# Ranked experts of a mixture layer in a mixed order: two-block places between three-block places

## The chip, the core and the metric

The kernel runs on one core of one Trainium2 chip, as one launch that computes the whole reference. The metric is device time in microseconds of that launch; the median of three runs stands for the kernel.

## The reference, cut to what matters

Two decoder layers run over 256 tokens of width 1024. Each has a mixer of three attention branches, a cross-attention, and a channel mixer. The channel mixer of the second layer is a mixture of 8 experts, of which each token uses the best 2:

```
logits = (t @ w_router)
top_val, top_idx = lax.top_k(logits, TOP_K)                  # TOP_K = 2
combine = sum(one_hot(top_idx, 8) * softmax(top_val)[..., None])
for e in range(8):
    out = out + combine[:, e:e+1] * (silu(t @ w_gate[e]) * (t @ w_up[e])) @ w_down[e]
```

Each expert has three float32 matrices: gate and up (1024 x 3584) and down (3584 x 1024), 42 MiB together. All 8 experts are needed, so 336 MiB are read in this part of the program, whatever the tokens do. A final RMSNorm ends the program.

## The kernel before

The first layer, the attention of both layers and the router come first. From about 757 us on, the program is the expert part, and this is the only part that the change touches.

**Places.** The experts are worked through in 8 places. Place 0 is always expert 0. The other seven experts are ranked by their number of tokens (order_experts: `place` is a count of the experts that have more), and places 1 to 7 take them by rank. A place has a fixed size, `CAPS[i]`: the first five places have room for 96 tokens (three blocks of 32), the last three for 64 (two blocks). If an expert had more tokens than its place, a loop behind the program's end (`overflow`) would compute the rest; otherwise it is skipped. The matrices of a place are found at run time: `ids` holds the expert's number, SyncE loads it into a register, and the DMA addresses are formed with it.

**One place.** An expert is worked in four groups of 1024, 1024, 1024 and 512 of the 3584 inner columns. `gate_up` (L962) multiplies the gathered tokens `hg` by the gate and up matrices into one PSUM bank per block (`ps_gu0` to `ps_gu2`): 96 matmul calls for a full group with three blocks, 64 with two. The profile has two records for each of these calls. ScalarE and VectorE form silu(gate) * up (`act_group`). `down` (L1000) multiplies the result of the group before by the down matrix into `ps_ey` (48 or 32 calls for a full group). So TensorE does gate/up of group g, then down of group g - 1, and so on across the border of two places. When the last down of a place is done, `scatter` (L1022) brings its result back to the token rows, in the middle of the next place's second group. `back` (L943, `ps_c`) makes the map for that, and `gather` (L916, `ps_hg`) picks the tokens of two places at a time, once for places 0 and 1, 2 and 3, 4 and 5, 6 and 7.

**The weights.** Each weight transfer moves a tile of 1 MiB (`raw`), 42 tiles for each place: per group 8 tiles for gate and up (4 in the last group) and 4 for down (2 in the last). All are issued by SyncE from one queue in one fixed order. The tiles live in 15 buffers, used in turn:

```
RAW1, RAW2, RAW3 = 3, 4, 8
    def raw_tile(self):
        pool = self.raws.pop(0)
        self.raws.append(pool)
        return pool.tile([P, 2048], F32, tag="raw", name="raw")
```

A transfer waits for two things: the last matmul that reads the tile 15 earlier must be done, and (eight semaphores in turn) the transfer 8 earlier must have landed. SyncE issues in order, so a waiting transfer holds all that are behind it. What the size of a place changes is how many matmuls read a tile, and so how soon its buffer comes free; the bytes are the same for each place.

Of the kernel before, what the change touches and what calls it, by code (L numbers as in the profile page):

```python
# [14 lines left out]
ALU = mybir.AluOpType  # L15
# [3 lines left out]
P = 128  # L19
D = 1024  # L20
KC = D // P
S = 256
# [8 lines left out]


TB = 32
CAPS = (96, 96, 96, 96, 96, 64, 64, 64)
BIG = sum(c == 96 for c in CAPS)

GROUPS = ((0, 1024), (1024, 1024), (2048, 1024), (3072, 512))

# [9 lines left out]
class Trunk:  # L48
# [744 lines left out]
    def numbers(self):  # L793

        m = N_EXP - 1
        self.num, self.numT = (self.rank.tile([P, m, m], F32, name=n) for n in ("num", "numT"))
        for a, p in ((self.num, [[0, m], [1, m]]), (self.numT, [[1, m], [0, m]])):
            self.nc.gpsimd.iota(a, pattern=p, base=1, channel_multiplier=0, allow_small_or_imprecise_dtypes=True)

    def order_experts(self, ps):  # L800

        nc = self.nc
        m = N_EXP - 1
        shape = [P, m, m]

        def small(name, shape=shape, dt=F32):
            return self.rank.tile(shape, dt, name=name)

        cnt = small("cnt", [P, N_EXP])
        nc.vector.tensor_copy(cnt, ps)  # L810
        lj = cnt[:, None, 1:].to_broadcast(shape)
        le = cnt[:, 1:, None].to_broadcast(shape)
        gt, eq = small("cgt"), small("ceq")
        nc.vector.tensor_tensor(gt, lj, le, op=ALU.is_gt)
        nc.vector.tensor_tensor(eq, lj, le, op=ALU.is_equal)
        nc.vector.tensor_tensor(eq, eq, self.lt[:, :m, :m], op=ALU.mult)
        nc.vector.tensor_tensor(gt, gt, eq, op=ALU.add)

        place = small("place", [P, N_EXP])
        nc.vector.memset(place[:, 0:1], 0.0)  # L820
        nc.vector.tensor_reduce(place[:, 1:], gt, axis=AX.X, op=ALU.add)
        nc.vector.tensor_scalar(place[:, 1:], place[:, 1:], 1.0, None, op0=ALU.add)

        self.at = small("at")
        nc.vector.tensor_tensor(self.at, place[:, None, 1:].to_broadcast(shape), self.numT, op=ALU.is_equal)
        self.pos2 = small("pos2", [P, NT, N_EXP])
        self.by_place(self.pos2, self.pos)
        ids = small("ids", [P, m])
        tmp = self.rank.tile(shape, F32, tag="bp", name="bp", bufs=2)
        nc.vector.tensor_tensor(tmp, self.at, self.num, op=ALU.mult)  # L830
        nc.vector.tensor_reduce(ids, tmp, axis=AX.X, op=ALU.add)
        self.ids = small("idi", [P, m], I32)
        nc.vector.tensor_copy(self.ids, ids)

        self.cap = small("cap", [P, N_EXP])
        nc.vector.tensor_scalar(self.cap, place, BIG - 0.5, -(CAPS[0] - CAPS[-1]), op0=ALU.is_gt, op1=ALU.mult)
        nc.vector.tensor_scalar(self.cap, self.cap, float(CAPS[0]), None, op0=ALU.add)
        nc.vector.tensor_tensor(cnt, cnt, self.cap, op=ALU.subtract)
        cm = small("cm", [P, 1])
        nc.vector.tensor_reduce(cm, cnt, axis=AX.X, op=ALU.max)  # L840
        nc.vector.tensor_scalar(cm, cm, float(CAPS[0]), None, op0=ALU.add)
        self.cnt = small("cnti", [P, 1], I32)
        nc.vector.tensor_copy(self.cnt, cm)
# [53 lines left out]
    def gather(self, i0):  # L897

        nc = self.nc
        caps = CAPS[i0:i0 + 2]  # L900
        n = sum(caps)
# [24 lines left out]
    def back(self, i):  # L926

        nc = self.nc
        big = CAPS[i] == 96
        m = 3 if big else 1  # L930
# [131 lines left out]
    def overflow(self, wg, wu, wd, out):  # L1062

        nc, tc = self.nc, self.tc
        n = nc.values_load(self.cnt[0:1, 0:1], min_val=0, max_val=S)
        with tc.If(n > CAPS[0]):
            with ExitStack() as st:
                sb = st.enter_context(tc.tile_pool(name="ov", bufs=1))
                raws = st.enter_context(tc.tile_pool(name="ovraw", bufs=2))
                ps1 = st.enter_context(tc.tile_pool(name="ovps1", bufs=2, space=PSUM))  # L1070
                ps2 = st.enter_context(tc.tile_pool(name="ovps2", bufs=1, space=PSUM))
                with tc.For_i(0, N_EXP, 1) as e:
                    for first in range(0, S - CAPS[-1], P):
                        self.overflow_expert(e, first, wg, wu, wd, sb, raws, ps1, ps2)
                    for a in (self.pos, self.cw, self.cap[:, None, :]):
                        tmp = sb.tile([P, NT, N_EXP - 1], F32, tag="shift", name="shift")[:, :a.shape[1]]
                        nc.vector.tensor_copy(tmp, a[:, :, 1:])
                        nc.vector.tensor_copy(a[:, :, :N_EXP - 1], tmp)
                self.finish(out)
# [191 lines left out]
```

## Time and profile before

| | |
|---|---|
| median of 3 runs | 1649.74 us (1647.7 to 1650.09) |
| profiled execution, own time | 1652.03 us |
| its span, first to last instruction | 1650.2 us |
| TensorE busy | 1591.9 us (96%) |
| VectorE, ScalarE, GpSimd busy | 621.3, 476.7, 72.0 us |
| DMA | 473.63 MB, mean 287 GB/s |

The busy share of TensorE is an average over the whole program, and a matmul's end in the profile is modelled: a TensorE that is 96% busy can still wait for weights in one part of the program. So the stretches have to be read one by one, and in each the rate of the transfers beside the work of TensorE.

### The profile page before, as it was taken

Reading aid. Unit: us, or ns where it says so; the run is one execution under the profiler, and the core shown is the slowest. Engines: PE = TensorE matmul, PEld = TensorE weight load, DVE = VectorE, ACT = ScalarE, POOL = GpSimd, SP = SyncE. Lnnn points to the kernel's source line nnn. Section 1 sums busy time; section 2 is a strip of 40 time slices with the busy share of each in tenths; the row PEclk is TensorE's granted clock in tenths of the full one; section 3 lists DMA queues with packets and bytes.
Section 4 is the critical chain, followed back from the end, with each engine's and each line's share of the span. In section 5 each row is a group of like instructions: output and inputs, shape, how many; then the busy total and the mean of one; then the engine's idle time right before and its main releaser. Section 6 shows DMA issues by size and latency. Waiting matters only on the chain.

```text
span 1650.2 us, 31391 instructions
## 1 busy us (share of the span) xinstructions
PE 1591.9 (96%) x13510; PEld 1003.7 (61%) x13510; DVE 621.3 (38%) x1150; ACT 476.7 (29%) x814; POOL 72.0 (4%) x106
## 2 busy tenths in 40 slices
PE   8999999999999999998999999999999999988885
PEld 7989998999999899973454343343343333322222
DVE  6656665655576666643212112202203122111111
ACT  6556556544455575532000000001001001000001
POOL 2003100000011021000000000000000000000000
PEclk9999999999999999997999999999999999999998
DMA  8445764655344355738999899998999999999996
GB/s 258 130 117 172 234 201 129 208 193 179 128 140 142 103 180 193 266 103 329 376 412 388 336 403 367 393 410 314 399 404 363 402 411 408 411 412 407 413 409 239
DMA packets 188768, 473.63 MB, mean 287 GB/s; under 512 B 8976, under 2 KB 99408, under 8 KB 174288
## 3 DMA queue, kind: packets, MB, share of 16 engines
q1 hardware_dynamic: 188592, 471.56, 76.7%
q8 instruction: 108, 1.77, 0.4%
q14 instruction: 36, 0.29, 0.1%
q10 hardware_dynamic: 32, 0.01, 0.0%
HBM read 470.49 MB, written 1.05 MB: 286 GB/s over the span
## 4 chain that ended last, share of the span: by engine, by line
PE 85%; DMA 13%; DVE 1%; ACT 0%; issue 0%; SPq 0%; POOL 0%; POOLq 0%; DVEq 0%; ACTq 0%
PE ps_gu L962 26%; PE ps_ey L1000 13%; DMA raw<-in_moe_up_dram 8%; DMA raw<-in_moe_down_dram 4%; PE ps_gate L127 3%; PE ps_gate L125 3%; PE ps_gate L126 3%; PE ps_fu L126 1%; PE ps_fg L126 1%; PE ps_fu L125 1%; PE ps_fg L125 1%; PE ps_fg L127 1%; PE ps_fu L127 1%; PE acc L125 1%; PE acc L126 1%; PE acc L127 1%
## 5 line engine op out<-in xcount | busy, mean ns | idle before, releaser
L962 PE MATMUL ps_gu<-raw,hg 128*32 128x512 f32 (+1 forms) x5376 | 572.3, 541 | 22.7 <-DMA raw<-in_moe_up_dram 18.3
L962 PEld LDWEIGHTS ps_gu<-raw,hg 128*32 128x32 f32 x5376 | 199.8, 110 | 362.7 <-issue 295.8
L74 DVE TENSOR_TENSOR wl<-raw,wh 128x1024 fp32r<-128x1024 f32 x214 | 268.3, 1262 | 159.3 <-ACT wh L72 159.2
L978 DVE TENSOR_TENSOR sl<-ps_gu,tmp 64x256 f32<-64x256 f32 (+1 forms) x168 | 66.2, 394 | 620.3 <-ACT tmp L974 617.9
L1000 PE MATMUL ps_ey<-raw,aT 128*32 128x512 f32 x2352 | 281.5, 593 | 7.0 <-DMA raw<-in_moe_down_dram 7.0
L72 ACT ACTIVATE wh<-raw 128x1024 fp32r<-128x1024 f32 x214 | 225.1, 1058 | 198.6 <-PE ps_gate L127 38.9
L974 ACT ACTIVATE tmp<-ps_gu 64x512 f32<-64x512 f32 (+1 forms) x84 | 44.9, 535 | 654.5 <-PE ps_gu L962 628.9
L1000 PEld LDWEIGHTS ps_ey<-raw,aT 128*32 128x32 f32 x2352 | 89.0, 110 | 175.7 <-issue 147.1
L127 PE MATMUL ps_gate<-tLmix,wh 128*128 128x256 f32 x384 | 109.3, 285 | 0.0
L125 PE MATMUL ps_gate<-tHmix,wh 128*128 128x256 f32 x384 | 109.2, 284 | 0.0
L126 PE MATMUL ps_gate<-tHmix,wl 128*128 128x256 f32 x384 | 108.8, 283 | 0.0
L127 PEld LDWEIGHTS ps_gate<-tLmix,wh 128*128 128x128 f32 x384 | 72.6, 189 | 2.1 <-issue 1.3
L126 PEld LDWEIGHTS ps_gate<-tHmix,wl 128*128 128x128 f32 x384 | 72.3, 188 | 1.0 <-issue 0.8
L125 PEld LDWEIGHTS ps_gate<-tHmix,wh 128*128 128x128 f32 x384 | 72.0, 188 | 0.9 <-issue 0.7
L126 PE MATMUL ps_fu<-tHffn,wl 128*128 128x256 f32 x176 | 49.9, 283 | 0.0
L126 PE MATMUL ps_fg<-tHffn,wl 128*128 128x256 f32 x176 | 49.9, 283 | 0.0
L127 PE MATMUL ps_fg<-tLffn,wh 128*128 128x256 f32 x176 | 49.7, 283 | 0.0
L127 PE MATMUL ps_fu<-tLffn,wh 128*128 128x256 f32 x176 | 49.7, 282 | 0.0
L125 PE MATMUL ps_fu<-tHffn,wh 128*128 128x256 f32 x176 | 49.6, 282 | 0.0
L125 PE MATMUL ps_fg<-tHffn,wh 128*128 128x256 f32 x176 | 49.5, 281 | 0.0
L979 DVE STREAM_TRANSPOSE aT<-sl 128x256 f32<-128x256 f32 (+1 forms) x84 | 47.7, 586 | 2.0
L1024 DVE SCALAR_TENSOR_TENSOR x<-ps_sc,cw,x 128x512 f32<-128x512 f32 x32 | 22.5, 747 | 54.2 <-PE ps_sc L1022 54.2
(388 smaller groups left out, 2376.3 us busy)
## 6 DMA issues: line engine op xcount, KB each, us to landing
raw<-in_moe_gate_dram SPq DMA_DIRECT2D x112, 1024.0 KB, 9.9
raw<-in_moe_up_dram SPq DMA_DIRECT2D x112, 1024.0 KB, 9.9
raw<-in_moe_down_dram SPq DMA_DIRECT2D x112, 1024.0 KB, 9.4
raw<-in_w_in_dram SPq DMA_DIRECT2D x41, 1024.0 KB, 5.3
raw<-in_ffn_gate_dram SPq DMA_DIRECT2D x11, 1024.0 KB, 5.4
raw<-in_ffn_up_dram SPq DMA_DIRECT2D x11, 1024.0 KB, 5.4
raw<-in_ffn_down_dram SPq DMA_DIRECT2D x11, 1024.0 KB, 4.9
raw<-in_w_mix_out_dram SPq DMA_DIRECT2D x8, 1024.0 KB, 5.2
```

Source lines behind the costliest of these rows:

```text
L72: a = nc.scalar.activation(wh, raw, AF.Copy)
L74: b = nc.vector.tensor_tensor(wl, raw, wh.bitcast(F32), op=ALU.subtract)
L125: ms = [nc.tensor.matmul(out, lh, rh, start=first, stop=False), nc.tensor.matmul(out, ll, rh, start=False, stop=False), nc.tensor.matmul(o ...
L126: nc.tensor.matmul(out, ll, rh, start=False, stop=False),
L127: nc.tensor.matmul(out, lh, rl, start=False, stop=last)]
L962: nc.tensor.matmul(ps[b][TB * q:TB * q + TB, :w].rearrange("p (s c) -> p s c", s=2), gT[:, k, TB * b:TB * b + TB], src[q // 2][:, k % nk, ...
L974: nc.scalar.activation(tmp[64:, :w], ps[b][:64, :w], AF.Silu)
L978: nc.vector.tensor_tensor(sl[64 * s:64 * s + 64, :w // 2], ps[b][64:, c], tmp[64:, c], op=ALU.mult)
L979: nc.vector.transpose(aT[:, :n, TB * b:TB * b + TB], sl[:, :w // 2].rearrange("p (r i) -> p i r", i=n))
L1000: nc.tensor.matmul(y[m][TB * q:TB * q + TB, :], aT[:, i0 + j, TB * b:TB * b + TB], raw[:, j * D + 512 * half:j * D + 512 * half + 512], st ...
L1024: nc.vector.scalar_tensor_tensor(xc, ps, self.cw2[:, t, i:i + 1], xc, op0=ALU.mult, op1=ALU.add)
```

## The change

The seven ranked places no longer take the ranks in falling order. A list gives the rank that each place takes, and the sizes follow the ranks: the four largest ranked experts (and expert 0) still have three blocks, the three smallest two.

```diff
-CAPS = (96, 96, 96, 96, 96, 64, 64, 64)
-BIG = sum(c == 96 for c in CAPS)
+RANKS = (4, 0, 1, 5, 2, 3, 6)
+BIG = 5
+CAPS = (96,) + tuple(96 if r < BIG - 1 else 64 for r in RANKS)
...
-        for a, p in ((self.num, [[0, m], [1, m]]), (self.numT, [[1, m], [0, m]])):
-            self.nc.gpsimd.iota(a, pattern=p, base=1, channel_multiplier=0, allow_small_or_imprecise_dtypes=True)
+        self.nc.gpsimd.iota(self.num, pattern=[[0, m], [1, m]], base=1, channel_multiplier=0,
+                            allow_small_or_imprecise_dtypes=True)
+        for i, r in enumerate(RANKS):
+            self.nc.gpsimd.memset(self.numT[:, i, :], r + 1.0)
...
-        nc.vector.tensor_scalar(self.cap, place, BIG - 0.5, -(CAPS[0] - CAPS[-1]), op0=ALU.is_gt, op1=ALU.mult)
+        nc.vector.tensor_scalar(self.cap, place, BIG - 0.5, -(CAPS[0] - min(CAPS)), op0=ALU.is_gt, op1=ALU.mult)
...
-                    for first in range(0, S - CAPS[-1], P):
+                    for first in range(0, S - min(CAPS), P):
```

The sizes of places 0 to 7 become 96, 64, 96, 96, 64, 96, 96, 64. The two-block places are now 1, 4 and 7 instead of 5, 6 and 7. `numT` is the table against which an expert's rank is compared to find its place; it is now filled row by row. The pairs that `gather` takes become 160, 192, 160 and 160 columns wide instead of 192, 192, 160 and 128.

On TensorE, at the first gate/up group of place 1, these rows stood before, behind the last down rows of place 0's third group (`ps_ey0` and `ps_ey1` are the two result banks of a three-block place, `raw` with a number is one weight tile, `hg` the gathered tokens):

```order
L1000 MATMUL ps_ey1_8481<-raw_9030,aT_8862 32x512 x4
L1000 MATMUL ps_ey0_8480<-raw_9030,aT_8862 32x512 x4
L962 MATMUL ps_gu0_9073<-raw_9076,hg_8270 32x512 x2
L962 MATMUL ps_gu0_9073<-raw_9078,hg_8270 32x512 x2
L962 MATMUL ps_gu1_9074<-raw_9076,hg_8270 32x512 x2
L962 MATMUL ps_gu1_9074<-raw_9078,hg_8270 32x512 x2
L962 MATMUL ps_gu2_9075<-raw_9076,hg_8270 32x512 x2
L962 MATMUL ps_gu2_9075<-raw_9078,hg_8270 32x512 x2
```

And these stand at the same point of TensorE's queue in the changed kernel:

```order
L1003 MATMUL ps_ey1_8487<-raw_9036,aT_8868 32x512 x4
L1003 MATMUL ps_ey0_8486<-raw_9036,aT_8868 32x512 x4
L965 MATMUL ps_gu0_9079<-raw_9081,hg_8276 32x512 x2
L965 MATMUL ps_gu0_9079<-raw_9083,hg_8276 32x512 x2
L965 MATMUL ps_gu1_9080<-raw_9081,hg_8276 32x512 x2
L965 MATMUL ps_gu1_9080<-raw_9083,hg_8276 32x512 x2
```

The third bank is gone: each weight tile of place 1 is read by two thirds of the matmuls.

At the first group of place 6, TensorE's queue before had these rows, behind the down rows of place 5, which has one result bank:

```order
L1000 MATMUL ps_ey0_12438<-raw_12867,aT_12760 32x512 x8
L1000 MATMUL ps_ey0_12438<-raw_12877,aT_12760 32x512 x8
L962 MATMUL ps_gu0_12910<-raw_12912,hg_12445 32x512 x2
L962 MATMUL ps_gu1_12911<-raw_12912,hg_12445 32x512 x2
L962 MATMUL ps_gu0_12910<-raw_12914,hg_12445 32x512 x2
L962 MATMUL ps_gu1_12911<-raw_12914,hg_12445 32x512 x2
```

In the changed kernel the same point of TensorE's queue, between places 5 and 6, reads:

```order
L1003 MATMUL ps_ey1_12030<-raw_12630,aT_12462 32x512 x4
L1003 MATMUL ps_ey0_12029<-raw_12630,aT_12462 32x512 x4
L965 MATMUL ps_gu0_12673<-raw_12676,hg_12037 32x512 x2
L965 MATMUL ps_gu1_12674<-raw_12676,hg_12037 32x512 x2
L965 MATMUL ps_gu2_12675<-raw_12676,hg_12037 32x512 x2
L965 MATMUL ps_gu0_12673<-raw_12678,hg_12037 32x512 x2
L965 MATMUL ps_gu1_12674<-raw_12678,hg_12037 32x512 x2
L965 MATMUL ps_gu2_12675<-raw_12678,hg_12037 32x512 x2
```

Places 5 and 6 now have the third block that places 1 and 4 gave up. SyncE's queue, with all 336 weight transfers, reads the same in both kernels row for row, and TensorE's queue is the same up to the first gather.

## Rows read from the trace of the kernel before

**Rows 1.** The page: TensorE's clock and transfer rate in 40 slices; the end chain.

```profile
PEclk9999999999999999997999999999999999999998
...
GB/s 258 130 117 172 234 201 129 208 193 179 128 140 142 103 180 193 266 103 329 376 412 388 336 403 367 393 410 314 399 404 363 402 411 408 411 412 407 413 409 239
...
PE 85%; DMA 13%; DVE 1%; ACT 0%; issue 0%; SPq 0%; POOL 0%; POOLq 0%; DVEq 0%; ACTq 0%
```

**Rows 2.** Windows: length, busy us by engine (instructions), TensorE clock, DMA share, GB/s.

```profile
745.00:761.00 16.00, 11.12 (x45) 6.96 (x44) 11.14 (x54) 5.03 (x11) 2.90 (x10) 0.50 0.83 321
900.00:925.00 25.00, 25.00 (x218) 10.50 (x214) 6.68 (x18) 4.32 (x9) 0.00 (x0) 1.00 0.73 264
925.00:1400.00 475.00, 475.00 (x4646) 172.66 (x4642) 87.84 (x187) 36.51 (x71) 0.00 (x0) 1.00 0.99 389
1400.00:1625.00 225.00, 196.39 (x1668) 64.16 (x1660) 31.14 (x64) 11.28 (x22) 0.00 (x0) 1.00 1.02 411
1125.00:1150.00 25.00, 25.00 (x186) 10.85 (x182) 5.81 (x12) 2.96 (x7) 0.00 (x0) 1.00 0.75 285
1500.00:1525.00 25.00, 18.72 (x216) 7.61 (x210) 2.04 (x6) 0.75 (x2) 0.00 (x0) 1.00 1.03 406
1625.00:1650.00 25.00, 9.88 (x73) 2.63 (x72) 5.96 (x9) 3.97 (x9) 3.58 (x5) 0.77 0.34 132
```

**Rows 3.** Timeline of TensorE, three-block places: start, length, line, count, idle before.

```profile
814.50 20.83 PE L962 MATMUL ps_gu<-raw,hg 128*32 128x512 f32 x192
835.10 10.53 PE L1000 MATMUL ps_ey<-raw,aT 128*32 128x512 f32 x96
845.40 10.59 PE L962 MATMUL ps_gu<-raw,hg 128*32 128x256 f32 x192
...
866.06 20.83 PE L962 MATMUL ps_gu<-raw,hg 128*32 128x512 f32 x192
886.66 5.38 PE L1000 MATMUL ps_ey<-raw,aT 128*32 128x512 f32 x48
...
895.41 0.97 PE L1022 MATMUL ps_sc<-yH,cT 128*128 128x512 f32 x3
...
1013.92 0.96 PE L1022 MATMUL ps_sc<-yH,cT 128*128 128x512 f32 x3
...
1128.24 0.97 PE L1022 MATMUL ps_sc<-yH,cT 128*128 128x512 f32 x3
```

**Rows 4.** Timeline of TensorE, first two-block place (place 5).

```profile
1380.74 13.92 PE L962 MATMUL ps_gu<-raw,hg 128*32 128x512 f32 x128
1394.48 7.05 PE L1000 MATMUL ps_ey<-raw,aT 128*32 128x512 f32 x64
1401.35 7.11 PE L962 MATMUL ps_gu<-raw,hg 128*32 128x256 f32 x128
```

**Rows 5.** Timeline of TensorE, places 6 and 7.

```profile
1440.50 0.73 PE L1022 MATMUL ps_sc<-yH,cT 64*128 64x512 f32 x3 [0.70 <-ACT yH L226]
...
1478.43 4.45 PE L962 MATMUL ps_gu<-raw,hg 128*32 128x512 f32 x32 [0.65 <-DMA raw<-in_moe_up_dram]
1483.54 4.46 PE L962 MATMUL ps_gu<-raw,hg 128*32 128x512 f32 x32 [0.66 <-DMA raw<-in_moe_up_dram]
...
1547.57 0.73 PE L1022 MATMUL ps_sc<-yH,cT 64*128 64x512 f32 x3 [0.70 <-ACT yH L226]
...
1632.83 1.92 PE L1000 MATMUL ps_ey<-raw,aT 128*32 128x512 f32 x16 [0.47 <-DMA raw<-in_moe_down_dram]
```

**Rows 6.** The tile raw on SyncE's queue, 950 to 975 us, then 1450 to 1500 us.

```profile
DMA to landing us min/median/max: 7.5/9.8/10.2
...
DMA to landing us min/median/max: 13.9/19.8/20.5
```

**Rows 7.** Waits of SyncE's queue, 690 to 1650 us: total us, times, longest.

```profile
SPq L113 <- PE ps_gu L962: 248.2, 72, 10.2
SPq L113 <- PE ps_ey L1000: 154.9, 83, 7.9
SPq L992 <- PE ps_gu L962: 142.8, 53, 5.9
```

**Rows 8.** The gathers in the chain that ended last: start, length, tile, count.

```profile
908.47 2.85 PE ps_hg L916 x24
...
1367.66 2.83 PE ps_hg L916 x24
```

**Rows 9.** Timeline of GpSimd around the number tables.

```profile
659.11 0.27 POOL L798 IOTA numT<- 128x49 f32 x1
694.12 1.06 POOL L173 TENSOR_TENSOR varcrs<-sscrs 128x2 f32<-128x2 f32 x1 [34.74 <-ACT junk L165]
```

## The prediction, made before the changed kernel was run

> **What bounds the kernel now.** I read the page's slices first. From the twentieth slice on (about 784 us) the transfer rate lies near 400 GB/s, with dips to 336, 367, 314 and 363 up to the thirty-first, and then, without a dip, at 402 to 413 [rows 1]. The chain that ended last puts 85% on TensorE and 13% on DMA [rows 1], so both matter, each in its own stretch. The windows show which where. From 925 to 1400 us TensorE is busy for all 475 us and the transfers run at 389 GB/s. From 1400 to 1625 us TensorE is busy for 196.39 of 225 us and the transfers run at 411 GB/s, with a share of 1.02 [rows 2]. The reader is to see two stages with different limits. In the three-block places TensorE is the bound and the transfers are held back; in the two-block places at the end the transfers are the bound and TensorE waits.
>
> The waits agree. SyncE's queue waited 248.2, 154.9 and 142.8 us for matmuls that still read a buffer [rows 7], and TensorE's waits for weights stand in the two-block places, 0.65 us and more ahead of each pair of tiles [rows 5].
>
> **Three speeds.** All follow from starts in the timelines.
> - A three-block place reads the 8 tiles of a gate/up group in 835.10 - 814.50 = 20.60 us, and 4 down tiles in 10.30 us [rows 3]: 2.575 us a tile, 42 x 2.575 = 108.2 us a place. With scatter, map and gather a place takes 1013.92 - 895.41 = 118.5 us, without a gather 1128.24 - 1013.92 = 114.3 us [rows 3]. So the side work is 6.1 us, and 4.2 us more with a gather.
> - A two-block place, when nothing is late, reads 8 tiles in 1394.48 - 1380.74 = 13.74 us and 4 in 6.87 us [rows 4]: 1.717 us a tile, 72.1 us a place. Its side work is between nothing and the 6.1 us of a three-block place: 72.1 to 78.2 us.
> - The transfers, when nothing holds them, bring 42 tiles in 1547.57 - 1440.50 = 107.07 us [rows 5]: 2.549 us a tile, which is 411 GB/s.
>
> So against the transfers a three-block place is 7.3 or 11.4 us too slow, and a two-block place 29 to 35 us too fast. What evens this out is the 15 buffers. In the three-block places a transfer lands 9.8 us after its issue [rows 6], which is 9.8 / 2.575 = 3.8 tiles; the other 11.2 tiles lie ready, worth 11.2 x 2.549 = 28.5 us of transfers. In the drained state it takes 19.8 us [rows 6], 7.8 tiles, and nearly nothing lies ready. Before, the buffers are full through five places and can store nothing more, while each scatter and gather stops the transfers (285 GB/s from 1125 to 1150 us [rows 2]). Then they drain once, and places 6 and 7 run at the transfers' pace.
>
> **The change part by part.**
>
> The order. Place 0 is as before, and its buffers are full. Place 1 has two blocks: it drains 29 to 35 us, about what is stored, so TensorE waits 0 to 6 us there. Places 2 and 3 give back 11.4 + 7.3 = 18.7 us, less than the 28.5 us of room, so the buffers never fill and no transfer is held back. Place 4 drains again, and TensorE waits 10 to 16 us; places 5 and 6 store 18.7 us again; place 7 drains and waits 10 to 16 us. From place 1 on, the transfers run without a stop. Then the time saved is the time in which they were held back before:
> - 925 to 1400 us: 475 x (1 - 389/411) = 25.4 us [rows 2]. Another count goes by tiles. What was moved after 925 us is 475 x 389 + 225 x 411 + 25 x 132 thousand bytes per microsecond [rows 2], less 1.6 MB of output and final gain: 279 MB, 266 tiles. At 2.549 us they need 678 us, and the last one was waited for until 1632.83 [rows 5], 707.8 us later: 29.5 us. That count holds the few microseconds between the last byte and the matmul, which stay. I take 25.4 and keep 29.5 as the bound.
> - 900 to 925 us: the dip at the border of places 0 and 1 costs 25 x (1 - 264/411) = 8.9 us [rows 2]. The first group of place 1 starts at 866.06 [rows 3] and will take 13.7 instead of 20.6 us, so 8 buffers come free 6.9 us earlier, and the transfers have that much queued when the dip comes. Between 6.7 and 8.9 us is saved; I take 8.0.
>
> The work of TensorE. Five places of three blocks and three of two: the same number of matmuls, scatters and maps. The gathers are 160, 192, 160, 160 wide instead of 192, 192, 160, 128; 24 of their matmuls take 2.85 us at 192 columns and 2.83 us at 128 [rows 8]. Nothing is gained or lost.
>
> The queues. SyncE's order is unchanged, so no transfer stands behind another that it did not stand behind before; only the moments at which buffers come free move. Of TensorE's queue the small moves of scatter calls by a few matmuls cost at most the 0.70 us for which `yH` was waited [rows 5] at seven borders, 0 to 5 us, and lie under the transfers: TensorE still has 20 to 38 us of waiting from places 1, 4 and 7.
>
> The tables. One iota of 0.27 us becomes seven fills. Bounded by that iota from above and zero from below they cost 0 to 1.9 us, of which nothing counts: GpSimd has nothing to do for 34.74 us behind it [rows 9]. Without that cover they would cost those 1.9 us once. The changed arguments of `cap` and of the loop have the same values as before.
>
> The sum: 25.4 + 8.0 = 33.4 us less. The profiled execution took 1652.03 us around a span of 1650.2 us, and I expect 1618.6 us of its like; from the median of 1649.74 us it gives **1616 us**, 2.0% less.
>
> The one value that all of this rests on is the rate that the transfers hold over 670 us. The trace has 411 GB/s over 225 us. By its nearest rows it could be 406 GB/s, as from 1500 to 1525 us [rows 2], or 413 GB/s, the best late slice [rows 1]. The 262 tiles left at 925 us then need 8.2 us more or 3.2 us less. The Trainium skill speaks against the change here: DMA: Bandwidth & Descriptors, "Where 436 GB/s comes from", says that for transfers from HBM the HBM side binds at about 358 GB/s for a core. By that figure the 262 tiles would take 767 us instead of 668, an estimate of about 1715 us. The trace disagrees: it shows 411 GB/s with this same kind of transfer, so the sum goes by the row.
>
> **The rivals.**
> - *The buffers fill up again.* If fewer tiles can lie ready than I count (the three pools take turns, and a late release in one holds the queue), the two pairs of three-block places are held back in their dips again, by about 8 us a pair. For it: 18.7 us of 28.5 us is no wide margin. Against it: in the last stretch the queue held its pace with the same turns. Time: 1616 + 16 = 1632 us.
> - *No change.* TensorE's work is the same and it is on 85% of the chain [rows 1]. If its waits at the end were only the modelled ends of matmuls and not lost time, the order would not matter: 1650 us. Against it: places 6 and 7 take 107 us where the same work can be done in 72 to 78 us [rows 4, 5].
> - *Slower: the clock.* Now that three-block places follow a drained queue, TensorE waits a little ahead of many pairs in places 2 and 5. From 745 to 761 us, where TensorE was busy for only 11.12 of 16 us, the granted clock was 0.50, the 1.2 GHz level [rows 2]. At that level a three-block place takes 108 us more. TensorE has 25 to 37 us of waiting left to cover it, and 33.4 us of gain to lose; a stretch of T us at half clock loses T/2, so it decides from about 120 to 140 us in all, more than one such place. One whole place takes 71 us or more from the sum: about 1690 us. Against it: in 1500 to 1525 us TensorE was busy for just 18.72 of 25 us, and the clock stayed at 1.00, as it did from 1400 to 1625 us as a whole [rows 2]. [...]
> - *The transfers do not hold their rate.* It needs less than 391 GB/s over the last 670 us to lose all the gain: 1650 us and more.
>
> **How the numbers follow.** The forecast has 0.80. Its own range goes from 1649.74 - (29.5 + 8.9 + 3.2) = 1608 to 1649.74 - (25.4 + 6.7 - 8.2) = 1626 us. Buffers that fill up again have 0.11, no change 0.05, the clock 0.03, the lower rate 0.01. The range takes the first two: 1608 to 1633 us. A measurement of this kernel can tell about 0.2% from no change, 3.3 us. Both the forecast and the first rival are faster: 0.91. No change is 0.05, slower 0.04.
>
> **What the profile would show.** Right: the rate stays at 406 to 413 GB/s in every window from about 900 us to the end, with no dip at a scatter; transfers land some 20 us after their issue from place 2 on; TensorE's waits for weights stand at places 4 and 7 and, in short ones, at the first pairs of 2 and 5; the last down matmuls start near 1599 us; the clock is 1.00 throughout. Wrong: dips at the borders of places 2 to 4 and 5 to 7 (the buffers filled), a window of three blocks with a clock under 1.00, or a rate near 390 GB/s although SyncE waits for no matmul.

## The result, and the profile after

The changed kernel takes 1620.27 us (median of 4 runs, 1620.21 to 1620.56), the kernel before 1649.91 us in the same measurement (4 runs, 1647.7 to 1650.21). The ratio is 0.9824, with a 95% interval of 0.9807 to 0.9841: 29.6 us less, 1.8%. The profiled execution took 1620.29 us around a span of 1618.6 us. The forecast was 1616 us, and 1618.6 us for a profiled execution.

The page of the changed kernel, the rows that answer to [rows 1]:

```profile
GB/s 254 142 110 176 213 232 105 205 194 195 162 96 139 131 138 202 286 157 192 380 407 412 406 412 411 409 409 414 406 412 403 412 412 400 410 413 401 413 407 228
...
PE 91%; DMA 7%; DVE 1%; ACT 0%; issue 0%; SPq 0%; POOL 0%; POOLq 0%; DVEq 0%; ACTq 0%
```

From the twenty-first slice to the last but one the transfers run at 400 to 414 GB/s. The dips to 336, 367, 314 and 363 of [rows 1] are gone. The stretch that answers to the idle time before, places 5 to 7, now has TensorE work for nearly all its time, so the chain that ended last lies more on TensorE (91% after 85%) although the kernel is nearer to the limit of the transfers. The chain goes back through whatever was released last; it does not say which resource has slack.

The windows of the changed kernel (length, busy us by engine with its instructions, TensorE clock, DMA share, GB/s), which answer to [rows 2]:

```profile
750.00:775.00 25.00, 23.58 (x170) 10.66 (x173) 7.26 (x34) 3.61 (x9) 0.00 (x0) 0.80 0.95 374
775.00:800.00 25.00, 24.54 (x228) 9.45 (x224) 5.16 (x11) 3.82 (x6) 0.00 (x0) 1.00 0.93 358
900.00:925.00 25.00, 25.00 (x230) 9.33 (x229) 4.86 (x13) 2.44 (x5) 0.00 (x0) 1.00 1.02 411
925.00:1350.00 425.00, 418.30 (x3918) 154.92 (x3914) 77.81 (x164) 32.36 (x63) 0.00 (x0) 1.00 1.02 410
1250.00:1260.00 10.00, 7.47 (x76) 3.35 (x80) 0.00 (x0) 0.00 (x0) 0.00 (x0) 0.83 1.02 388
1350.00:1375.00 25.00, 25.00 (x241) 9.79 (x237) 4.40 (x9) 1.77 (x3) 0.00 (x0) 1.00 1.01 391
1450.00:1475.00 25.00, 25.00 (x240) 8.21 (x238) 3.56 (x7) 0.59 (x1) 0.00 (x0) 1.00 1.02 395
925.00:1594.00 669.00, 657.48 (x6304) 246.93 (x6300) 120.72 (x254) 49.64 (x96) 0.00 (x0) 1.00 1.02 409
```

The border of places 0 and 1, 900 to 925 us, went from 264 to 411 GB/s, and the 669 us behind it hold 409 GB/s as a whole. Two windows stand out, 391 and 395; they come back below.

The waits of SyncE's queue from 690 to 1620 us (total us, times, longest), the same three groups as [rows 7]:

```profile
SPq L114 <- PE ps_gu L965: 207.3, 77, 10.6
SPq L114 <- PE ps_ey L1003: 102.2, 55, 7.0
SPq L995 <- PE ps_gu L965: 83.8, 44, 5.9
```

Before, they were 248.2, 154.9 and 142.8 us. They don't fall to zero, and need not: a wait of the queue costs nothing so long as enough transfers are already under way. How many there are shows in the time from issue to landing. The tile `raw` on SyncE's queue, from 950 to 975 us, then from 1450 to 1500 us, as in [rows 6]:

```profile
DMA to landing us min/median/max: 18.7/20.2/20.3
...
DMA to landing us min/median/max: 12.0/14.2/14.4
```

At 950 to 975 us it was 9.8 us and is 20.2. From 1450 to 1500 us, now late in the second pair of three-block places, it is 14.2 us where it was 19.8. The median goes to and fro over the program (20.2, 15.1 from 1100 to 1200 us, 20.0 from 1225 to 1250, 14.2), as it should where full and empty buffers take turns.

TensorE's last down matmuls in the timeline (start, length, line, tile, count, idle before), against [rows 5]:

```profile
1601.06 1.92 PE L1003 MATMUL ps_ey<-raw,aT 128*32 128x512 f32 x16 [0.48 <-DMA raw<-in_moe_down_dram]
```

The last down matmuls start at 1601.06 instead of 1632.83 us, 31.8 us earlier. That is the difference of the two profiled executions, 1652.03 - 1620.29 = 31.7 us: the whole gain lies ahead of this row.

### The profile page after: what moved, and what is told of

It is laid out like the page before. It is cut to its first block, busy times and chain, and to the rows that moved or that the text cites. A ratio compares the mean times of both kernels' runs of the same rounds, so it can differ in the third digit from the quotient of the medians.

```text
span 1618.6 us, 31395 instructions
## 1 busy us (share of the span) xinstructions
PE 1576.6 (97%) x13510; PEld 1011.9 (63%) x13510; DVE 621.3 (38%) x1150; ACT 477.0 (29%) x814; POOL 72.2 (4%) x112
## 4 chain that ended last, share of the span: by engine, by line
PE 91%; DMA 7%; DVE 1%; ACT 0%; issue 0%; SPq 0%; POOL 0%; POOLq 0%; DVEq 0%; ACTq 0%
PE ps_gu L965 30%; PE ps_ey L1003 14%; PE ps_gate L128 3%; PE ps_gate L126 3%; PE ps_gate L127 3%; DMA raw<-in_moe_down_dram 3%; DMA raw<-in_moe_up_dram 2%; PE ps_sc L1025 1%; PE ps_fu L127 1%; PE ps_fg L127 1%; PE ps_fu L126 1%; PE ps_fg L126 1%; PE ps_fg L128 1%; PE ps_fu L128 1%; PE acc L126 1%; PE acc L127 1%
## 5 line engine op out<-in xcount | busy, mean ns | idle before, releaser
L965 PE MATMUL ps_gu<-raw,hg 128*32 128x512 f32 (+1 forms) x5376 | 563.4, 542 | 7.7 <-DMA raw<-in_moe_up_dram 4.7
L965 PEld LDWEIGHTS ps_gu<-raw,hg 128*32 128x32 f32 x5376 | 207.1, 110 | 332.2 <-issue 296.5
```

The lines of the kernel that those rows point to most:

```text
L965: nc.tensor.matmul(ps[b][TB * q:TB * q + TB, :w].rearrange("p (s c) -> p s c", s=2), gT[:, k, TB * b:TB * b + TB], src[q // 2][:, k % nk, ...
```

## The experiments

The theory: the time saved is that in which the transfers were held back by full buffers, so it depends on where the three-block places stand in relation to what the buffers can store. The rivals differ by run: that only the place of some two-block places matters, that TensorE's waits cost nothing, or that the number of buffers doesn't matter. The kernels of one group ran on one chip, beside the kernel before: e1 to e4 beside a median of 1649.61 us, e5 to e8 of 1650.67, e10 and e11 of 1650.08, e12 of 1650.39.

### Four orders

**e1: one two-block place early, two at the end.**

```diff
-RANKS = (4, 0, 1, 5, 2, 3, 6)
+RANKS = (4, 0, 1, 2, 3, 5, 6)
```

> Two-block places at 1, 6 and 7: of the three moves only one is made, place 5's goes to place 1. Theory (the gain is the time in which the transfers were held back by full buffers): after place 1 has drained them, places 2 to 5 give back 11.4 + 7.3 + 11.4 + 7.3 = 37 us against about 28 us of room, so only some 6 to 9 us are held back again: about 1627 us (1624 to 1631). Rival (each two-block place that is set between three-block places brings its share of the 29.6 us): about a third, 1640 us.

Measured: 1628.83 us, ratio 0.9876 (0.986 to 0.9893). Its windows:

```profile
900.00:1200.00 300.00, 299.30 (x2910) 112.64 (x2907) 52.85 (x116) 22.43 (x44) 0.00 (x0) 1.00 1.02 410
1200.00:1300.00 100.00, 100.00 (x1004) 36.21 (x1000) 20.71 (x44) 8.49 (x16) 0.00 (x0) 1.00 1.01 402
1300.00:1400.00 100.00, 100.00 (x936) 36.76 (x932) 19.19 (x39) 8.84 (x17) 0.00 (x0) 1.00 0.95 369
1400.00:1600.00 200.00, 185.91 (x1680) 64.59 (x1675) 32.19 (x67) 12.25 (x24) 0.00 (x0) 0.99 1.02 410
```

Place 1 ends at 975.65 us, by the first matmul of its scatter, and the three-block places 2 to 5 at 1092, 1215, 1328 and 1437 us. Up to 1200 us, in places 2 and 3, nothing is held back; after that 100 x (1 - 402/411) + 100 x (1 - 369/411) = 12.4 us are lost, most of them in the fourth three-block place of the run. That fits the theory's time, and the rate falls where the stored room should be used up. The four places together, from the first matmul of place 2 to that of place 6, stand in these two rows:

```profile
948.57 21.66 PE L965 MATMUL ps_gu<-raw,hg 128*32 128x512 f32 x186
...
1416.23 13.94 PE L965 MATMUL ps_gu<-raw,hg 128*32 128x512 f32 x128
```

They take 467.7 us, 39.4 more than 168 tiles at 2.549 us (the expectation had 37). So the room was 39.4 - 12.4 = 27.0 us, 10.6 tiles, where the prediction's count has 28.5 us, 11.2 tiles. It may be somewhat more: TensorE waited for no weights in place 1, so something may still have lain ready at its end.

**e2: two- and three-block places in turn, a three-block place last.**

```diff
-RANKS = (4, 0, 1, 5, 2, 3, 6)
+RANKS = (0, 4, 1, 5, 2, 6, 3)
```

> Two-block places at 2, 4 and 6: strictly alternated, but the first one comes a place later and a three-block place ends the program. Theory: places 0 and 1 hold the transfers back as before (about 9 us at the first dip, 5 to 7 us in place 1), and what lies ready when place 7 starts is not used up by a two-block place: 12 to 18 us slower than the mixed order, about 1635 us. Rival (what counts is how evenly the sizes are alternated): 1620 us or less.

Measured: 1642.16 us, ratio 0.995 (0.9934 to 0.9967). "More evenly mixed" is not what counts: this is the most even order of all and gains 7 us. Two of its windows:

```profile
900.00:1000.00 100.00, 100.00 (x1012) 37.91 (x1006) 16.98 (x42) 8.29 (x17) 0.00 (x0) 1.00 0.95 367
...
1590.00:1620.00 30.00, 30.00 (x380) 13.72 (x376) 2.90 (x9) 1.12 (x3) 0.00 (x0) 1.00 0.58 233
```

Place 1 has three blocks while the buffers are full, and loses 100 x (1 - 367/411) = 10.7 us. At the end the transfers run out before 1620 us and TensorE still has the stored tiles of a three-block place to work through. The direction was the theory's; the time missed its 1635 us by 7. Some 4 us of that may be the late load of the final gain, by what e11 shows for the order of e3; it was not run in this order.

**e3: all two-block places first.**

```diff
-RANKS = (4, 0, 1, 5, 2, 3, 6)
+RANKS = (4, 5, 6, 0, 1, 2, 3)
```

> Two-block places at 1, 2 and 3, none behind them. Theory: the transfers run freely through places 1 to 3, but TensorE waits there for some 60 us as it did at the end of the sorted order, the buffers fill in places 4 to 6, and the end is TensorE's: about 1645 us (1641 to 1651), close to the sorted order. Rival (one early drain is what counts): about 1620 to 1627 us.

Measured: 1655.53 us, ratio 1.0036 (1.0023 to 1.0049), slower than the sorted order. Two of its windows, and then the load of the final gain in its trace (line, count, length in ns, when):

```profile
1400.00:1500.00 100.00, 100.00 (x958) 34.51 (x954) 17.41 (x33) 7.37 (x13) 0.00 (x0) 1.00 1.01 399
...
1590.00:1620.00 30.00, 30.00 (x380) 12.54 (x376) 5.93 (x14) 2.89 (x6) 0.00 (x0) 1.00 0.44 173
```

```profile
L1149 SPq DMA_DIRECT2D gbf<-in_final_norm_dram x1: 338/338/338, 1638.2 to 1638.2; - x1
```

The rival's 1620 to 1627 us is excluded, but the theory missed as well: it had 1645 us (1641 to 1651), a little below the sorted order, and the run lies 6 us above that order. The transfers run at 409 GB/s from 900 to 1400 us, then fall to 399 and, from 1500 to 1590 us, to 390, and end near 1603 us; TensorE works on until 1637 us with nothing left to transfer. So time at the full transfer rate alone is not the measure: what is stored at the end is work that no transfer hides. The last row shows one more thing, unforeseen: the final gain `gbf` is loaded only at 1638.2 us, behind the last scatter, because its tile takes memory of the places. With a two-block place last it is issued at 1583.2 us.

**e4: all places with two blocks.** This leaves out the third block, a third of the matmuls of places 0, 2, 3, 5 and 6, so tokens beyond 64 of an expert are not computed.

```diff
-CAPS = (96,) + tuple(96 if r < BIG - 1 else 64 for r in RANKS)
+CAPS = (64,) * 8
...
-        with tc.If(n > CAPS[0]):
+        with tc.If(n > 96):
```

> All eight places have two blocks, so a third of the expert matmuls of five places are left out (about 5 x 36 us of TensorE's work), and tokens beyond 64 of an expert are left out of the result; the limit at which the loop behind the end would run is set to 96 so that it is skipped as before. The bytes are the same. Theory: the mixed order is already at the pace of the transfers from the first places on, so 180 us less work for TensorE gives almost nothing: 1615 to 1620 us, transfers at 408 to 413 GB/s throughout. Rival (TensorE, on 91% of the chain that ended last, is still the bound): tens of us less, under 1600 us.

Measured: 1612.97 us, ratio 0.9779 (0.9763 to 0.9795). With 5 x (108.2 - 72.1) = 180 us of TensorE's work less, by the speeds of [rows 3, 4], only 7.3 us are to be had beyond the mixed order. Its windows show the limit:

```profile
750.00:800.00 50.00, 47.50 (x400) 19.55 (x404) 12.59 (x41) 6.67 (x14) 0.00 (x0) 0.91 1.03 413
...
925.00:1350.00 425.00, 372.99 (x3012) 122.06 (x3016) 62.46 (x132) 24.04 (x48) 0.00 (x0) 0.99 1.02 410
```

From 925 to 1350 us the rate is the mixed order's 410 GB/s, with TensorE idle for 52 us instead of 6.7. The difference stands at 750 to 800 us: 413 GB/s against the 374 and 358 above, worth 50 x (413 - 366)/411 = 5.7 us. That is place 0, in which the buffers fill for the first time, and the change doesn't touch it.

### The number of buffers

**e6: the changed kernel once more**, as the base for e5 and e7. No edit.

> The mixed order as changed, once more on the same chip as the others of this set: 1620 us by each theory.

Measured: 1621.13 us, ratio 0.9821 (0.9807 to 0.9834).

**e7 and e8: 9 buffers**, in the mixed and in the sorted order.

```diff
-RAW1, RAW2, RAW3 = 3, 4, 8
+RAW1, RAW2, RAW3 = 3, 4, 2
```

> The mixed order with 9 buffers (the third pool has 2 tiles). Theory: some 5 tiles can lie ready, 13 us of transfers; a pair of three-block places gives back 18.7 us, so the buffers fill in both pairs and the transfers are held back there again, and fewer tiles are ahead when place 1 starts: about 22 us more than with 15, 1642 us. Rival (alternating the sizes is enough by itself): as much more as the sorted order loses with 9 buffers.

> The sorted order of before with 9 buffers. Theory: in the three-block places TensorE is the bound as before; six tiles fewer lie ready when the two-block places start, 6 x 2.55 = 15 us: about 1665 us, so that the gain of the mixed order shrinks from 30 to some 22 us. Rival: the same loss in both orders, the gain stays at 30 us.

Measured: the mixed order 1656.55 us, ratio 1.0036 (1.0023 to 1.0049); the sorted one 1665.84 us, ratio 1.0096 (1.0081 to 1.0112). The gain of the mixed order falls from 1650.67 - 1621.13 = 29.5 us to 9.3 us. The theory had e8 right and put e7 at 1642 us; the rival, that the room for tiles is not what counts, would have kept the gain. Neither size was right, but the gain does shrink with the buffers. The windows of e7:

```profile
1100.00:1200.00 100.00, 100.00 (x968) 37.62 (x961) 22.53 (x48) 9.49 (x19) 0.00 (x0) 1.00 0.93 362
1200.00:1300.00 100.00, 88.58 (x782) 31.32 (x773) 15.89 (x32) 5.87 (x11) 0.00 (x0) 1.00 1.02 411
...
1300.00:1475.00 175.00, 174.30 (x1588) 65.07 (x1586) 30.88 (x64) 14.40 (x28) 0.00 (x0) 1.00 0.98 384
```

In the first pair of three-block places the transfers lose 100 x (1 - 362/411) = 11.9 us, in the second 175 x (1 - 384/411) = 11.5 us. The first pair as a whole, places 2 and 3, goes from the first of these rows to the second:

```profile
963.71 21.97 PE L965 MATMUL ps_gu<-raw,hg 128*32 128x512 f32 x186 [0.72 <-DMA raw<-in_moe_gate_dram]
...
1200.31 0.62 PE L965 MATMUL ps_gu<-raw,hg 128*32 128x512 f32 x3
```

It takes TensorE 236.6 us, 22.5 more than 84 tiles at 2.549 us; the prediction's working has 18.7. So the room was about 22.5 - 11.9 = 10.6 us, 4.2 tiles, and by the second pair (237.2 us) 4.5 tiles. The prediction's count, buffers less the 3.8 tiles under way, has 9 - 3.8 = 5.2. That is up to a tile too many, as in e1: it counts as room what is about to be read or just being read as well, which would explain it and has no run of its own. With 15 buffers, then, some 27 us of room stand against 22 to 23 us that a pair asks for: a margin of some 4 us instead of the prediction's 9.8. The theory's 13 us of room and 18.7 us a pair would have lost 5.7 us in each; what was lost beyond that accounts for some 12 of the 14.5 us by which it missed e7.

**e5: 16 buffers** (RAW3 = 9).

> The mixed order with 16 instead of 15 weight buffers (the third pool has 9 tiles). Theory: one more tile can lie ready, so the small dips in places 5 and 6 (391 and 395 GB/s for 25 us each, some 2 us in all) go away and one more transfer is issued when place 0 starts: 2 to 5 us less than the mixed order with 15. Rival (in the mixed order the buffers' number no longer matters, since the transfers never wait for them): no change, within 1 us.

Measured: 1622.06 us, ratio 0.9826 (0.9813 to 0.984), no gain over e6, as the rival had it. But its last scatter starts at 1601.0 us, 2.5 us ahead of e6's 1603.5, and then the end takes 18.7 us of span instead of 15.2. The waits of SyncE's queue show what took it back:

```profile
SPq L1149 <- DVE yL L228: 23.1, 1, 23.1
SPq L1149 <- PE ps_sc L1025: 2.1, 1, 2.1
```

L1149 loads the final gain. With one buffer more its tile lies where the last scatter's `yL` is, so the load waits for it and lands behind it. That is the same late load as in e2 and e3. Three runs tested it. A fourth, e9, has no result: it is e12 with two buffers in the pool `ch`, and one of its pools needs 14 kB of a partition where 10.3 kB are left.

**e10 to e12: the final gain in a tile of its own.** e10 is the mixed order with 15 buffers, e11 the order of e3, e12 the mixed order with 16 buffers.

```diff
-        self.gbf = self.fin.tile([P, D], F32, name="gbf")
+        self.gbf = self.rt.tile([P, D], F32, name="gbf")
```

In e12 also, to make room:

```diff
-RAW1, RAW2, RAW3 = 3, 4, 8
+RAW1, RAW2, RAW3 = 3, 4, 9
...
-            k.ch = pool(p3, "ch", 2)
+            k.ch = pool(p3, "ch", 1)
```

> The mixed order with 15 buffers and the final gain in its own tile, as a control: nothing of the places moves. With 15 buffers the load of the gain was not on the last chain, so 1620 to 1621.5 us. Should it come to 1618.5 us, the gain's load cost the mixed order as well and e9 says nothing of the buffer.

> The two-block places at 1, 2 and 3 with the final gain in its own tile. In e3 the load of the gain waited until the last scatter, and the stretch from the last scatter's first matmul to the end took 19.1 us in the orders that end on a three-block place, 15 us in those that end on a two-block one. If the late gain makes that difference, it falls by about 4 us to 1651.5 us (1650.5 to 1653). If the larger scatter of a three-block place makes it, it stays at 1655.5 us.

> The mixed order with 16 buffers and the final gain in its own tile. To make room the 0/1 matrices of the gathers and scatters (pool ch) have one buffer instead of two; each is made once in a place, long after the one before it was read, so this should add no wait. Nothing is left out. If the 16th buffer really brings 2.5 us and the late load of the gain took it back, the last scatter comes some 2.5 us earlier than with 15 buffers and the time is about 1618 us (1617 to 1619.5), against 1620.5 us of the control with 15. If a 16th buffer brings nothing in the places, it stays at 1620 to 1622 us.

Measured: e10 1620.52 us, ratio 0.982 (0.9806 to 0.9833), no change, as expected of the control. e11 1651.88 us, ratio 1.0013 (1.0004 to 1.0022), 3.7 us under e3 (on another chip; the intervals of the ratios do not touch): the late gain cost about that much, and the early block does not get below the sorted order without it either. e12 1618.01 us, ratio 0.9804 (0.979 to 0.9818): 2.5 us under e10, on the same chip, and 4.1 and 3.1 us under e5 and e6, on another. It is the fastest kernel that leaves nothing out. Its interval and e10's overlap, but each of its five runs lies below each of e10's five. The stretches from the last scatter to the end of the span fit: 15.7 us in e11 (e3: 18.9), 15.5 us in e12 (e5: 18.7), 14.7 us in e10. One window of e10, then two of e12:

```profile
750.00:800.00 50.00, 47.48 (x390) 20.27 (x394) 13.56 (x51) 8.43 (x16) 0.08 (x1) 0.90 0.97 382
...
750.00:800.00 50.00, 49.10 (x402) 20.86 (x406) 11.56 (x39) 7.68 (x16) 0.00 (x0) 0.91 1.01 403
...
1450.00:1475.00 25.00, 25.00 (x240) 8.21 (x234) 0.67 (x2) 0.00 (x0) 0.00 (x0) 1.00 1.02 395
```

The sixteenth buffer works in place 0, where the buffers fill for the first time: 403 GB/s against 382, worth 50 x 21/411 = 2.6 us. e5 against e6, both without the gain's tile, has 387 against 370 GB/s there, 2.1 us. The smaller pool `ch` of e12 has no run of its own. The small dip at 1450 to 1475 us is still there at 395.

## Why the prediction was right, step by step

**The case.** The forecast's case came true: the transfers now run almost without a stop from place 1 on, and the time is 1620.3 us, inside the forecast's own 1608 to 1626 us. e1 and e7 show the mechanism from two sides: with too many three-block places in a row, or with too few buffers, the transfers are held back again and the time follows. e4 shows that it is the transfers that bound what is left. Two signs held only in part: of the 27 windows of 25 us from 900 to 1575 us five have less than 406 GB/s, 391 and 395 the lowest, and the transfers land after some 20 us at the start of each pair of three-block places but after 14 to 15 us late in it.

**The dip at 900 to 925 us.** Taken as 8.0 us, with 8.9 as its bound. The window now has 411 GB/s, so all 8.9 us came back.

**The time held back from 925 to 1400 us.** This is the term that was mis-sized. 25.4 us was taken, as if not one microsecond stayed. From 925 to 1594 us the rate is 409 and not 411 GB/s: 669 x (1 - 409/411) = 3.3 us stayed. So 25.4 + 8.9 - 3.3 = 31.0 us, against 31.8 between the two rows of the last down matmuls and 33.4 in the sum. The other 0.8 us was there before the change could act: the row of place 0 that starts at 814.50 us in [rows 3] starts 0.9 us earlier in this trace.

```profile
813.58 20.84 PE L965 MATMUL ps_gu<-raw,hg 128*32 128x512 f32 x192
```

The other count of this term, 29.5 us in the prediction, is 707.8 - 678 = 29.8 us by its own numbers; nothing hangs on the difference.

**Where those 3.3 us are.** About 2.2 of them lie in the windows 1350 to 1375 and 1450 to 1475 us, in the second pair of three-block places. SyncE's queue at the first (start, length of the wait with the issue, line), and the windows of 5 us that follow it:

```profile
1345.41 10.01 SPq L114 DMA_DIRECT2D raw<-in_moe_gate_dram  x1
```

```profile
1350.00:1355.00 5.00, 5.00 (x52) 2.01 (x48) 0.00 (x0) 0.00 (x0) 0.00 (x0) 1.00 1.01 399
1355.00:1360.00 5.00, 5.00 (x52) 1.96 (x48) 0.00 (x0) 0.00 (x0) 0.00 (x0) 1.00 0.95 338
1360.00:1365.00 5.00, 5.00 (x52) 1.86 (x46) 0.00 (x0) 0.54 (x1) 0.00 (x0) 1.00 1.04 380
```

One transfer stood 10 us for a matmul, and the rate fell to 338 and 380 GB/s right behind it. The queue was held back as in the first rival, but in small, at 3 us instead of 16. Whether the buffers were full as a whole, or one buffer's late release held the queue while others were free, is not settled. Against full buffers speaks that from 1375 to 1450 us, further into the pair, the rate was 410 to 412 GB/s again, and that the sixteenth buffer of e12 left the dips at 398 and 395 GB/s, where e10 with 15 has 398 and 397. But e12 had also brought more tiles ahead by then.

**TensorE's waits.** Here the working was off, though the sum makes no use of it. It expected 0 to 6 us of waiting in place 1 and 10 to 16 us in each of places 4 and 7, 20 to 38 us together. From 887 to 1604 us the matmuls that read weights waited for transfers for 7.2 + 4.6 = 11.8 us (busy us, mean ns, idle before):

```profile
L965 PE MATMUL ps_gu<-raw,hg 128*32 128x512 f32 (+1 forms) x4456 | 470.7, 540 | 7.2 <-DMA raw<-in_moe_up_dram 4.7 <-DMA raw<-in_moe_gate_dram 2.5
L1003 PE MATMUL ps_ey<-raw,aT 128*32 128x512 f32 x2016 | 244.0, 593 | 4.6 <-DMA raw<-in_moe_down_dram 4.6
```

None of it lies in place 1, 5.3 us in place 4 and 6.5 us in place 7. Two sizes in the working were off, both towards less waiting. From the first matmul of a place's first group to that of the next place's, place 1 takes 83.4 us, and places 2 and 3 together 236.4 us, all without a wait for weights (starts of places 1, 2 and 4):

```profile
865.14 13.97 PE L965 MATMUL ps_gu<-raw,hg 128*32 128x512 f32 x128
...
948.58 21.81 PE L965 MATMUL ps_gu<-raw,hg 128*32 128x512 f32 x186
...
1185.01 0.62 PE L965 MATMUL ps_gu<-raw,hg 128*32 128x512 f32 x3
```

So a two-block place drains 107.07 - 83.4 = 23.7 us and not 29 to 35, and a pair of three-block places gives back 236.4 - 214.1 = 22.3 us and not 18.7. The 72.1 to 78.2 us of the working come from a place's own tiles and at most 6.1 us of side work. But place 1 also holds a gather (the first of [rows 8]), and the last down tiles and the scatter of the three-block place before it. The trace of before shows that already: its place 5, with a gather and behind a three-block place, takes 84.2 us without a wait for weights (starts of places 5 and 6):

```profile
1330.94 0.61 PE L962 MATMUL ps_gu<-raw,hg 128*32 128x512 f32 x3
...
1415.12 1.89 PE L962 MATMUL ps_gu<-raw,hg 128*32 128x512 f32 x8
```

The gather is not the whole of it: place 4 of the changed kernel, which has none, takes 88.8 us, 83.5 without its waits. Of the pair of three-block places, place 3 takes 121.0 us where the working has 118.5 for a place with a gather. The moved scatter calls may be the cause; no run shows it by itself. The transfers stayed the bound, so the time did not suffer. But the waiting that was to cover a lower clock or late scatter calls was some 12 us and not 20 to 38.

**From the profile to the median.** The other 2 us or so of the miss are no term of the kernel. The profiled execution of before lay 2.3 us above its median (1652.03 and 1649.74), and the sum was taken from the median as if that of the changed kernel would lie as high. It lies on its median: 1620.29 and 1620.27 us. Profile against profile the forecast of 1618.6 us was 1.7 us off.

**What was hidden.** The seven fills left no mark that a row shows: the row at 813.58 us above comes no later than before. What the moved scatter calls may have cost TensorE lies under the transfers.

**The rivals.** *Buffers fill up again*: held back in small, above; in full in e1 and e7, with other orders or fewer buffers. *No change*: excluded; TensorE's waits before were lost time. *The transfers lose their rate*: 409 GB/s over 669 us, so no. The rule of the Trainium skill that stood against the change (DMA: Bandwidth & Descriptors, "Where 436 GB/s comes from", with 358 GB/s for a core from HBM) is not borne out by this trace of a launch on one core, which has 409. *The clock*: the prediction's "1.00 throughout" was wrong in one place, and cost nothing. In the window from 1250 to 1260 us the granted clock is 0.83: a third of the window at the 1.2 GHz level, some 3.4 us. It is place 4, drained as foreseen, and the timeline there shows TensorE waiting for the transfers (last column):

```profile
1247.67 1.92 PE L1003 MATMUL ps_ey<-raw,aT 128*32 128x512 f32 x16 [0.41 <-DMA raw<-in_moe_down_dram]
1250.17 1.92 PE L1003 MATMUL ps_ey<-raw,aT 128*32 128x512 f32 x16 [0.58 <-DMA raw<-in_moe_down_dram]
1252.93 1.06 PE L965 MATMUL ps_gu<-raw,hg 128*32 128x256 f32 x8 [0.83 <-DMA raw<-in_moe_gate_dram]
1255.51 8.35 PE L965 MATMUL ps_gu<-raw,hg 128*32 128x256 f32 x114 [1.53 <-DMA raw<-in_moe_up_dram]
```

TensorE had been waiting for weights and waited for them again right after, 0.56 us at 1268.55 us, so it lost time that it would have waited anyway; the transfers stayed at 409 GB/s over 1200 to 1300 us. From 775 to 1600 us no other stretch shows a clock under 1.00, so no three-block place behind place 0 lost any of it, which is what the rival needed.

## What to carry to other kernels

Where stages bound by compute and stages bound by transfers follow one another on one ring of buffers, put their order down as a balance: each compute stage fills the ring by so many microseconds, each transfer stage drains it by so many, and what goes over the brim or below the bottom is lost. Order the stages so that the balance stays inside what the ring can store, start draining when it is full, and end on a draining stage, since what is stored at the end is compute that nothing hides: the even alternation (e2) lost most of the gain and the early block (e3) all of it, largely on these two points; a late load at the end (e11) was some 4 us of it in e3. Read a stage's length from its start to the start of the next, with all the side work in it. Of the ring, count as room somewhat less than the buffers that are not under way, and after every change of buffers look at what else moved in memory: a load of the program's last stage can become late by it (e5), and is then given its own tile (e12).

## What the runs showed of the hardware that was not expected

- One core drew 409 GB/s from HBM over 669 us in a row, with TensorE busy for 657.48 us of it; the compute took nothing from the transfers. e4 has 410 GB/s with TensorE at 88%.
- The clock fell to the 1.2 GHz level for some 3.4 us in place 4, behind waits of 0.41, 0.58, 0.83 and 1.53 us between short pieces of matmuls. In place 7, waits of 0.85, 1.54 and 1.63 us between such pieces left it at 1.00; what makes the difference no run shows. The window from 1575 to 1600 us and the rows of these waits:

```profile
1575.00:1600.00 25.00, 19.07 (x224) 7.69 (x224) 2.02 (x6) 0.75 (x2) 0.00 (x0) 1.00 0.92 367
```

```profile
1577.91 1.06 PE L965 MATMUL ps_gu<-raw,hg 128*32 128x256 f32 x8 [0.85 <-DMA raw<-in_moe_gate_dram]
1580.51 3.76 PE L965 MATMUL ps_gu<-raw,hg 128*32 128x256 f32 x64 [1.54 <-DMA raw<-in_moe_up_dram]
1585.90 3.00 PE L965 MATMUL ps_gu<-raw,hg 128*32 128x256 f32 x50 [1.63 <-DMA raw<-in_moe_up_dram]
```

- During a single stop of SyncE's queue for 10 us, from 1345 to 1355 us, the rate was 410 GB/s; it fell to 338 and 380 GB/s in the two windows of 5 us after it. Transfers issued around there (1340 to 1380 us) landed 13.6 to 21.5 us after their issue, so tiles under way can have covered the stop itself.
